# Attention scores for two heads at a time, and two weight chunks split ahead of a layer's last products: a two-block decoder on one Trainium2 core

## The chip, the core and the metric

The kernel runs as one program on one core of a Trainium2 chip. The metric is device time in microseconds (us), from the start of the program to its end. Below, TensorE is PE in the profile, VectorE is DVE, ScalarE is ACT, GpSimd is POOL, and SP is the engine whose queue issues the transfers.

## What is computed

256 tokens of width 1024 go through two blocks in float32. The first block is a mixer of three branches (short convolution, stick-breaking attention, retention), an attention over a memory of 256 rows and a squared-ReLU MLP. The second block has two layers with post-layer-norm: layer 0 is a state-space mixer and a convolutional FFN, layer 1 a latent attention (MLA) and the same kind of FFN. The parts that the change touches are the latent attention, the output products that end each sub-layer, and the norms behind them:

```python
def mla_shared_kv(h, kv_down_proj, kv_norm_g, kv_up_k, kv_up_v, cos, sin):
    ckv_kr = h @ kv_down_proj
    c_kv = rms_norm(ckv_kr[..., :MLA_KV_RANK], kv_norm_g)
    k_rope = apply_rope(ckv_kr[..., MLA_KV_RANK:], cos, sin)
    k_nope = (c_kv @ kv_up_k).reshape(b, s, 8, 128)
    v = (c_kv @ kv_up_v).reshape(b, s, 8, 128)

# for each block of 128 queries:
        scores = (jnp.einsum('bqhd,bkhd->bhqk', qn, k_nope)
                  + jnp.einsum('bqhr,bkr->bhqk', qr, k_rope)).astype(jnp.float32) * scale
        scores = jnp.where(key_idx[None, :] <= q_idx[:, None], scores, -jnp.inf)
        p = jax.nn.softmax(scores, axis=-1).astype(v.dtype)
        return jnp.einsum('bhqk,bkhd->bqhd', p, v)

def layer_norm(x, g, b):
    mu = jnp.mean(xf, axis=-1, keepdims=True)
    var = jnp.mean(jnp.square(xf - mu), axis=-1, keepdims=True)
    return (xf - mu) * lax.rsqrt(var + LN_EPS) * g + b
```

A score has a part over 128 features of its own head (nope) and a part over 64 rotary features whose keys all heads share (rope).

## The kernel before

**Tiles.** The 256 tokens are two token tiles (tau = 0 and 1) of 128. A float32 product is made of three products in fp32r: high part of the activations by high part of the weights, high by low, low by high (`mm3`, from line 672). In the profile these operands are `ah`, `al` (or `oTh`, `oTl`, `gTh`, `gTl`) and `wh`, `wl`.

**The weight stream.** The weights come as chunks in a fixed order. A chunk is transferred into `wr` (two buffers, `RAW`), ACT makes its high part with a CAST `wh<-wr` in two halves (`copy`, from line 523), and DVE makes its low part with a TENSOR_TENSOR `wl<-wr,wh`, again in two halves (`sub`, from line 537). When the second half is subtracted, the raw buffer is free, and `pump` issues the next transfer. Up to four prepared chunks are held (`HELD`): `can_prep` lets a chunk be split when it is transferred and fewer than four chunks lie between it and the last one that PE is done with. `get` hands a chunk to the products, `done` gives it back; `n_get`, `n_prep` and `n_done` count them.

**The order of the work** is settled when the program is built. A planner with a clock of its own runs the kernel's generators as tasks: `tick`, called between products, steps the tasks whose inputs it reckons ready, tasks marked `first` ahead of others, and `split_next` puts casts and subtractions between them, on the engine's reckoned idle time. What comes out is one list of instructions for each engine, and each engine takes its list in order. So an instruction that waits holds all that stands behind it on its engine.

**Layer ends.** `xstat` (from line 715) makes products whose moving side are the weights: output tiles of 128 tokens by up to 512 columns in two column blocks. The chunks that are not in the tail are used for both token tiles at once. The tail chunks (the last 2 to 4, `TAIL`) are used for tau 0 in a row, then for tau 1 in a row; in the last tail chunk the column blocks are done one after the other, and after block 0 a task is spawned that takes the result: `layernorm` (line 902) or an RMS norm. `layernorm` does, for each of two halves of 512 columns, a DVE SCALAR_TENSOR_TENSOR `x<-x,mm` (residual) and an ACT ACTIVATE `tk<-x,ln` (squares), then small DVE steps, a power on POOL, and two DVE SCALAR_TENSOR_TENSOR `x<-tk,rs,gb`; then PE transposes (`sm<-cst,x`, four to a PSUM bank), ACT casts them to `ah` and DVE subtracts to `al`. These two feed the next stage.

`xstat` with a task behind it ends six times: `wo` (after the mixers), `xo` (after the memory attention), `down` (after the MLP), `fd` (after the FFN of layer 0, and again of layer 1), `kvq` (the down projections of the latent attention, four chunks of 2 x 128 rows by 704 columns) and `ao` (its output). The next stage after `xo` is `up`, after layer 0's `fd` it is `kvq`, after `ao` it is `fu` (the FFN's first products). `up` and `fu` begin with three chunks that are used for tau 0, then for tau 1 (`wmixed`).

**Attention scores.** In `attention` (line 1784) each of the eight heads is a task `head(i)` (line 1924). It takes one PSUM bank of the `sm` group (four banks), makes the nope products (`sm<-knT,qnT`), adds the causal mask by two products (`sm<-maskb,identb`), makes the rope products, which use 64 of the 128 rows of the array (`sm<-krT,qrT`; even heads lie in rows 0 to 63, odd heads in rows 64 to 127), and then does the softmax on DVE and ACT, three transposes of `p`, and the product with `v`. Four heads are spawned after the query products of the first weight chunk, four after the second. `before(c)` holds chunk c of `ao` back until the heads of that chunk are done.

Nearly all instructions are recorded under one line, 284, that of a helper.

Of the kernel before, what the change touches and what calls it, by code (L numbers as in the profile page):

```python
# [471 lines left out]
class Kern:  # L472
# [86 lines left out]
    def done(self):  # L559
        self.n_done += 1  # L560

    def now(self):
# [155 lines left out]
    def xstat(self, tag, nks, lhs, blocks, tail=0, after=None, before=None):  # L720
# [29 lines left out]
        if tail:  # L750
            chs = []
            for tau in range(2):
                kk = k0
                if tau and ps[1] is None:
                    ps[1] = [self.bank() for _ in blocks]
                for c in range(tail):
                    if tau == 0:
                        if before:
                            before(len(nks) - tail + c)
                        chs.append(self.get(tag))  # L760
                    nk = nks[len(nks) - tail + c]
                    if c == tail - 1 and after:
                        got = [0]
                        for n in every:
                            part(chs[c], nk, kk, tau, [n])
                            got[0] += 1
                            if n == 0:
                                self.spawn(after(tau, ps[tau], got), first=True)
                            elif n < len(blocks) - 1:
                                self.tick()  # L770
                    else:
                        part(chs[c], nk, kk, tau, every)
                    kk += nk
                    if tau:
                        self.done()
                    else:
                        self.skew = 0.0 if c == tail - 1 else self.skew + nk * chs[c][0].shape[2] * UNIT / 2
                    self.tick()
# [1005 lines left out]
    def attention(self, h, act):  # L1784
# [4 lines left out]
        krT = pool.tile([P, S], F32, tag="krT", name="krT")  # L1789
        knT = pool.tile([P, 8, S], F32, tag="knT", name="knT")  # L1790
        qnT = pool.tile([P, 8, S], F32, tag="qnT", name="qnT")
        qrT = pool.tile([P, 4, S], F32, tag="qrT", name="qrT")
# [7 lines left out]
        for n, o in (("kvn", 0), ("qn", 256)):  # L1800
            b, w = ROWS[n]
# [119 lines left out]
        scale = 192 ** -0.5  # L1921
        obank = {}

        def head(i):
            sc = yield from self.sm.wait()
            r = slice(64 * (i % 2), 64 * (i % 2) + 64)
            self.mm1(sc[:, 0:128], qnT[:, i, 0:128], knT[:, i, 0:128], True)
            self.mm1(sc[:, 128:384], qnT[:, i, 128:256], knT[:, i, :], False)
            self.mm1(sc[:, 0:128], self.identb, self.maskb, False)
            self.mm1(sc[:, 256:384], self.identb, self.maskb, False)  # L1930
            self.mm1(sc[:, 0:128], qrT[r, i // 2, 0:128], krT[r, 0:128], False)
            self.mm1(sc[:, 128:384], qrT[r, i // 2, 128:256], krT[r, :], False)
            yield "dve"
            mx = self.tiny.tile([P, 2], F32, tag="mx", name="mx")
            nc.vector.tensor_reduce(mx[:, 0:1], sc[:, 0:128], axis=AX.X, op=MAX)
# [23 lines left out]
            c = slice(P * i, P * i + P)  # L1959
# [4 lines left out]
            yield from self.split((oT[0][:, i, :], oT[1][:, i, :]), po[:, :256])  # L1964
            self.sm.put(po)

        hs = []
        for b in (0, 4):
            self.wstat("qn", cq, 3, evac_to(qnT, b))
            self.until(*g_qr, *g_v)  # L1970
            for i in range(b, b + 4):
                hs.append(self.spawn(head(i)))
                self.tick()
        g_, b_ = self.bcast("lmg1", self.gb, "gb"), self.bcast("lmb1", self.gb, "gb")
        act = self.new_act()

        def before(c):
            self.until(*hs[:2 * c + 2])
        ps = self.xstat("ao", [2] * 4, self.lhs(oT), [(0, 512), (512, 1024)], tail=TAIL["ao"], before=before,
                        after=lambda t, p, got: self.layernorm(t, h, g_, b_, act, p, got))  # L1980
        close()
# [106 lines left out]
```

## Time and profile before

| | before |
|---|---|
| time, median of 3 runs | 1234.38 us (1233.92 to 1234.63) |
| the profiled execution: its own time | 1233.43 us |
| the profiled execution: its span | 1231.7 us |
| PE busy | 1214.2 us (99%) |
| DVE busy | 852.7 us (69%) |
| ACT busy | 718.0 us (58%) |
| all waits of PE on other work, as listed | 9.0 us |

The span runs from the first to the last instruction; 1.7 us of the execution's time lie outside it. The profiled execution is 0.95 us below the median of the runs. The busy time of PE is the union of its instructions, which overlap: a product of 256 columns is recorded with 0.28 us, and the next starts 0.117 us later.

### The profile page before, as it was taken

To read this page: it belongs to the slowest core of one execution; us is meant where nothing else is said; L and a number is where in the kernel's file an instruction comes from. 1 tells how busy PE (TensorE), PEld (TensorE's weight loads), DVE (VectorE), ACT (ScalarE), POOL (GpSimd) and SP (SyncE) were. 2 spreads that over 40 slices of the span, in tenths; PEclk is the share of its full clock that TensorE was granted. 3 is DMA by queue.
4 is the path that set the end of the run, shared out by engine and by line. 5 is a ranking of instruction groups with operands and counts; after the bars stand their busy time and mean duration, and the time that the engine had idled before them with its cause. 6 is when DMAs were issued, how large, how long until landed. Compare 5 with 4: busy or idle time off the path is not lost.

```text
span 1231.7 us, 20769 instructions
## 1 busy us (share of the span) xinstructions
PE 1214.2 (99%) x8468; PEld 1109.8 (90%) x8468; DVE 852.7 (69%) x1378; ACT 718.0 (58%) x1181; POOL 53.2 (4%) x85
## 2 busy tenths in 40 slices
PE   7999999999999999999999999999999999999997
PEld 5979999989989998888999898999988888999986
DVE  5666848677747765446887797888855866888853
ACT  5666546446536554345789765666643665666631
POOL 0011000000000000000111201000000000000000
PEclk9999999999999999999999999999999999999999
DMA  7643355546444556524556545555673442455560
GB/s 257 246 159 132 142 198 221 185 163 227 172 154 167 211 193 226 183 105 172 224 206 237 190 172 197 180 185 193 216 262 105 164 184 106 171 206 190 209 251 34
DMA packets 35425, 227.71 MB, mean 185 GB/s; under 512 B 4321, under 2 KB 4993, under 8 KB 11522
## 3 DMA queue, kind: packets, MB, share of 16 engines
q1 hardware_dynamic: 35330, 226.39, 51.1%
q8 instruction: 66, 1.08, 0.3%
q14 instruction: 29, 0.24, 0.1%
HBM read 225.27 MB, written 1.10 MB: 184 GB/s over the span
## 4 chain that ended last, share of the span: by engine, by line
PE 93%; DVE 3%; DMA 1%; ACT 1%; issue 0%; POOL 0%; SPq 0%; POOLq 0%; DVEq 0%; ACTq 0%
PE mm L284 84%; PE sm L284 9%; DMA wr<-wts 1%; DVE wl L284 1%; DVE x L284 1%; DVE tk L284 0%; POOL rs L284 0%; ACT wh L284 0%; SPq L284 0%; DVE dtw L284 0%; DVE ln L284 0%; DVE al L284 0%; ACT L284 0%; ACT tk L284 0%; POOLq L2084 0%
## 5 line engine op out<-in xcount | busy, mean ns | idle before, releaser
L284 DVE TENSOR_TENSOR wl<-wr,wh 128x1024 fp32r<-128x1024 f32 (+3 forms) x408 | 478.7, 1196 | 174.2 <-ACT wh L284 173.5
L284 ACT CAST wh<-wr 128x1024 fp32r<-128x1024 f32 (+3 forms) x408 | 403.9, 1030 | 160.4 <-PE mm L284 88.6
L284 PE MATMUL mm<-ah,wh 128*128 128x256 f32 (+1 forms) x1496 | 417.1, 279 | 0.0
L284 PE MATMUL mm<-ah,wl 128*128 128x256 f32 (+1 forms) x1496 | 413.6, 276 | 0.1
L284 PE MATMUL mm<-al,wh 128*128 128x256 f32 (+1 forms) x1496 | 413.4, 276 | 0.0
L284 PEld LDWEIGHTS mm<-ah,wh 128*128 128x128 f32 (+1 forms) x1496 | 280.2, 187 | 1.6 <-issue 1.1
L284 PEld LDWEIGHTS mm<-al,wh 128*128 128x128 f32 (+1 forms) x1496 | 280.3, 187 | 0.4
L284 PEld LDWEIGHTS mm<-ah,wl 128*128 128x128 f32 (+1 forms) x1496 | 280.2, 187 | 0.4 <-DVE wl L284 0.3
L284 DVE SCALAR_TENSOR_TENSOR r<-mm,pcol,r 128x255 f32<-128x255 f32 (+2 forms) x212 | 86.9, 474 | 35.1 <-ACT r L284 35.1
L284 PE MATMUL mm<-wl,ah 128*128 128x512 f32 (+3 forms) x320 | 106.1, 338 | 3.0 <-DVE wl L284 2.9
L284 PE MATMUL mm<-wh,ah 128*128 128x512 f32 (+3 forms) x320 | 108.7, 346 | 0.0
L284 PE MATMUL mm<-wh,al 128*128 128x512 f32 (+3 forms) x320 | 106.3, 338 | 0.5 <-DVE al L284 0.5
L284 PE MATMUL mm<-wh,gTh 128*128 128x512 f32 x304 | 96.2, 391 | 0.0
L284 PE MATMUL mm<-wl,gTh 128*128 128x512 f32 x304 | 95.6, 389 | 0.0
L284 PE MATMUL mm<-wh,gTl 128*128 128x512 f32 x304 | 95.5, 389 | 0.0
L284 ACT ACTIVATE r<-mm,pcol 128x256 f32<-128x256 f32 x96 | 48.9, 560 | 43.3 <-PE mm L284 43.3
L284 PEld LDWEIGHTS mm<-wl,ah 128*128 128x128 f32 x320 | 60.4, 190 | 10.0 <-DVE wl L284 4.6
L284 PEld LDWEIGHTS mm<-wh,gTl 128*128 128x128 f32 x304 | 57.1, 188 | 11.9
L284 PEld LDWEIGHTS mm<-wl,gTh 128*128 128x128 f32 x304 | 57.1, 188 | 11.8
L284 PEld LDWEIGHTS mm<-wh,gTh 128*128 128x128 f32 x304 | 56.7, 188 | 12.0 <-issue 0.6
L284 PEld LDWEIGHTS mm<-wh,al 128*128 128x128 f32 x320 | 60.2, 189 | 7.0 <-DVE al L284 1.2
L284 PEld LDWEIGHTS mm<-wh,ah 128*128 128x128 f32 x320 | 60.3, 189 | 6.5 <-issue 0.7
(296 smaller groups left out, 1576.6 us busy)
## 6 DMA issues: line engine op xcount, KB each, us to landing
wr<-wts SPq DMA_DIRECT2D x186, 1024.0 KB, 4.8
wr<-wts SPq DMA_DIRECT2D x11, 768.0 KB, 4.3
gb<-prow SPq DMA_DIRECT2D x12, 512.0 KB, 6.5
dec<-rows SPq DMA_DIRECT2D x8, 768.0 KB, 8.1
wr<-wts SPq DMA_DIRECT2D x4, 704.0 KB, 4.1
wr<-wts SPq DMA_DIRECT2D x4, 512.0 KB, 6.5
tk<-mem SPq DMA_DIRECT2D x2, 512.0 KB, 7.3
out<-x SPq DMA_DIRECT2D x4, 256.0 KB, 2.1
```

Source lines behind the costliest of these rows:

```text
L284: r = f(*args, **kw)
```

## The change

**Splits at layer ends.** A new function `ahead(n)` splits chunks at once, without the planner's rule on idle time, until n chunks beyond the one last handed out are prepared, or none can be. `xstat` calls `ahead(2)` in tau 1 in front of the last tail chunk's products, where a task follows. At the end of layer 1's `fd` no chunk is left, and at the end of `kvq` the order of the weight splits stays as it was.

**Scores.** Two heads become one task `scores(j)`. It waits for two `sm` banks, makes the nope products of both heads, then the masks of both, then the rope products of both, alternating between the two row groups. The two softmaxes are spawned as tasks `head(i, sc)` behind that.

The number of PE products is the same. Elsewhere (memory attention, the state-space mixer) the planner also puts some instructions in another order.

```diff
+    def ahead(self, n):
+
+        while self.n_prep < min(self.n_get + n, self.nch) and (self.subs or self.can_prep()):
+            self.sub() if self.subs else self.copy()
@@ xstat
                     if c == tail - 1 and after:
+                        if tau:
+                            self.ahead(2)
                         got = [0]
@@ attention
-        def head(i):
-            sc = yield from self.sm.wait()
-            r = slice(64 * (i % 2), 64 * (i % 2) + 64)
-            self.mm1(sc[:, 0:128], qnT[:, i, 0:128], knT[:, i, 0:128], True)
-            self.mm1(sc[:, 128:384], qnT[:, i, 128:256], knT[:, i, :], False)
-            self.mm1(sc[:, 0:128], self.identb, self.maskb, False)
-            self.mm1(sc[:, 256:384], self.identb, self.maskb, False)
-            self.mm1(sc[:, 0:128], qrT[r, i // 2, 0:128], krT[r, 0:128], False)
-            self.mm1(sc[:, 128:384], qrT[r, i // 2, 128:256], krT[r, :], False)
+        def scores(j):
+
+            scs = yield from self.sm.wait(2)
+            for e, sc in enumerate(scs):
+                i = 2 * j + e
+                self.mm1(sc[:, 0:128], qnT[:, i, 0:128], knT[:, i, 0:128], True)
+                self.mm1(sc[:, 128:384], qnT[:, i, 128:256], knT[:, i, :], False)
+            for sc in scs:
+                self.mm1(sc[:, 0:128], self.identb, self.maskb, False)
+                self.mm1(sc[:, 256:384], self.identb, self.maskb, False)
+            for q, k, o in ((slice(0, 128), slice(0, 128), slice(0, 128)), (slice(128, 256), slice(0, 256), slice(128, 384))):
+                for e, sc in enumerate(scs):
+                    r = slice(64 * e, 64 * e + 64)
+                    self.mm1(sc[:, o], qrT[r, j, q], krT[r, k], False)
+            for e, sc in enumerate(scs):
+                hs[2 * j + e] = self.spawn(head(2 * j + e, sc))
+
+        def head(i, sc):
             yield "dve"
...
-        hs = []
+        hs, pairs = {}, []
...
-            for i in range(b, b + 4):
-                hs.append(self.spawn(head(i)))
+            for j in range(b // 2, b // 2 + 2):
+                pairs.append(self.spawn(scores(j)))
...
         def before(c):
-            self.until(*hs[:2 * c + 2])
+            self.until(*pairs[:c + 1])
+            self.until(*[hs[i] for i in range(2 * c + 2)])
```

**Where layer 0 ends and `kvq` begins.** On ACT, the kernel before has the following. The `wh<-wr` casts of 704 columns are halves of `kvq`'s chunks, the `tk,ln<-x,ln` are the two squares of the layer norm of tau 1, and `ah` are the casts behind the transposes.

```order
L284 CAST wh<-wr 128x704 x3
L284 ACTIVATE ln<-ln 128x1
L284 ACTIVATE tk_9734,ln<-x,ln 128x512 x2
L284 ACTIVATE ln<-ln 128x1
L284 CAST wh<-wr 128x704 x2
L284 CAST ah<-sm_9808 128x4x128
L284 CAST ah<-sm_9818 128x4x128
L284 CAST wh<-wr 128x704 x2
```

And after the change, also on ACT:

```order
L284 CAST wh<-wr 128x704 x3
L284 ACTIVATE ln<-ln 128x1
L284 ACTIVATE tk_9735,ln<-x,ln 128x512
L284 CAST wh<-wr 128x704 x2
L284 ACTIVATE tk_9735,ln<-x,ln 128x512
L284 ACTIVATE ln<-ln 128x1
L284 CAST ah<-sm_9815 128x4x128
L284 CAST wh<-wr 128x704 x2
L284 CAST ah<-sm_9832 128x4x128
```

The two casts of `kvq`'s third chunk now stand between the two squares, and those of the fourth chunk ahead of the second `ah`.

On PE at the same place, the kernel before has this. `mm_9762` and its neighbour are the output of `kvq` for tau 0, and `sm<-cst,x` are the eight transposes of the layer norm of tau 1.

```order
L284 MATMUL mm_9762<-wl,ah 128x320
L284 MATMUL mm_9763<-wl,ah 128x384
L284 MATMUL mm_9762<-wh,al 128x320
L284 MATMUL mm_9763<-wh,al 128x384
L284 MATMUL sm_9808<-cst,x 128x128 x4
L284 MATMUL sm_9818<-cst,x 128x128 x4
L284 MATMUL mm_9762<-wh,ah 128x320
L284 MATMUL mm_9763<-wh,ah 128x384
L284 MATMUL mm_9762<-wl,ah 128x320
```

And after the change, from the first products of the third chunk on:

```order
L284 MATMUL mm_9766<-wh,ah 128x320
L284 MATMUL mm_9767<-wh,ah 128x384
L284 MATMUL mm_9766<-wl,ah 128x320
L284 MATMUL mm_9767<-wl,ah 128x384
L284 MATMUL mm_9766<-wh,al 128x320
L284 MATMUL mm_9767<-wh,al 128x384
L284 MATMUL sm_9815<-cst,x 128x128 x4
L284 MATMUL mm_9766<-wh,ah 128x320
L284 MATMUL mm_9767<-wh,ah 128x384
L284 MATMUL mm_9766<-wl,ah 128x320
```

Six products of the third chunk now stand ahead of the first four transposes, and six more ahead of the other four.

**Where `ao` ends and `fu` begins.** On DVE, the kernel before has this from the layer norm of tau 0 (its last two steps `x<-tk`) to that of tau 1. The `wl<-wr,wh` are halves of `fu`'s first chunks (those of the first one stand further ahead).

```order
L284 SCALAR_TENSOR_TENSOR x<-tk_10567,rs,gb 128x512 x2
L284 TENSOR_TENSOR al<-sm_10610,ah 128x4x128
L284 TENSOR_TENSOR al<-sm_10623,ah 128x4x128
L284 TENSOR_TENSOR wl<-wr,wh 128x1024
L284 SCALAR_TENSOR_TENSOR x,ln<-x,mm_10489 128x512
L284 TENSOR_TENSOR wl<-wr,wh 128x1024
L284 SCALAR_TENSOR_TENSOR x,ln<-x,mm_10490 128x512
```

And after the change, also on DVE:

```order
L284 SCALAR_TENSOR_TENSOR x<-tk_10557,rs,gb 128x512 x2
L284 TENSOR_TENSOR wl<-wr,wh 128x1024 x2
L284 TENSOR_TENSOR al<-sm_10614,ah 128x4x128
L284 TENSOR_TENSOR al<-sm_10621,ah 128x4x128
L284 TENSOR_TENSOR wl<-wr,wh 128x1024 x2
L284 SCALAR_TENSOR_TENSOR x,ln<-x,mm_10483 128x512
L284 SCALAR_TENSOR_TENSOR x,ln<-x,mm_10484 128x512
```

Four subtractions of weights now stand between the end of the one layer norm and the first residual step of the other, where one stood.

## Rows read from the trace of the kernel before

**Rows 1.** Page, part 1: busy time, share of the span, instructions

```profile
PE 1214.2 (99%) x8468; PEld 1109.8 (90%) x8468; DVE 852.7 (69%) x1378; ACT 718.0 (58%) x1181; POOL 53.2 (4%) x85
```

**Rows 2.** Waits of PE: total us, times, longest us

```profile
PE mm L284 <- DVE wl L284: 2.9, 3, 1.8
```

**Rows 3.** Timeline of PE, head scores (start, us, operation, tile, shape, [idle before])

```profile
989.88 0.82 PE L284 MATMUL sm<-knT,qnT 128*128 128x128 f32 x4
990.53 0.28 PE L284 MATMUL sm<-maskb,identb 128*128 128x128 bf16 x2
990.74 0.92 PE L284 MATMUL sm<-krT,qrT 64*128 64x128 f32 x4
991.59 0.92 PE L284 MATMUL sm<-knT,qnT 128*128 128x128 f32 x4
```

**Rows 4.** Timeline of PE, scores of two heads of the first block's attention

```profile
47.87 0.92 PE L284 MATMUL sm<-qT,kT 64*128 64x256 f32 x8
48.72 0.50 PE L284 MATMUL mm<-wh,ah 128*128 128x512 f32 x1
```

**Rows 5.** Timeline of DVE, end of the first head's softmax

```profile
993.94 0.55 DVE L284 TENSOR_SCALAR p<-p,sm 128x128 f32<-128x128 f32 x2
```

**Rows 6.** Timeline of ACT, end of layer 0

```profile
950.51 0.72 ACT L284 ACTIVATE tk<-x,ln 128x512 f32<-128x512 f32 x1 [0.36 <-DVE x L284]
...
951.42 1.45 ACT L284 CAST wh<-wr 128x704 fp32r<-128x704 f32 x2
```

**Rows 7.** Timeline of SP, end of layer 0: issue of the third kvq chunk

```profile
947.18 0.33 SPq L284 DMA_DIRECT2D wr<-wts  x1
```

**Rows 8.** Page, part 6: count, KB each, median us from issue to landing

```profile
wr<-wts SPq DMA_DIRECT2D x186, 1024.0 KB, 4.8
...
wr<-wts SPq DMA_DIRECT2D x4, 704.0 KB, 4.1
```

**Rows 9.** Timeline of DVE, end of layer 0

```profile
953.09 1.41 DVE L284 SCALAR_TENSOR_TENSOR x<-tk,rs,gb 128x512 f32<-128x512 f32 x2 [0.44 <-POOL rs L284]
...
957.22 1.68 DVE L284 TENSOR_TENSOR wl<-wr,wh 128x704 fp32r<-128x704 f32 x2
```

**Rows 10.** Timeline of PE, start of kvq

```profile
953.89 1.38 PE L284 MATMUL sm<-cst,x 128*128 128x128 f32 x8 [0.34 <-DVE x L284]
...
958.96 0.42 PE L284 MATMUL mm<-wl,ah 128*128 128x320 f32 x1
```

**Rows 11.** Timeline of DVE, end of the memory attention (xo)

```profile
377.02 1.42 DVE L284 SCALAR_TENSOR_TENSOR tk<-x,rs,gb 128x512 f32<-128x512 f32 x2 [0.73 <-POOL rs L284]
```

**Rows 12.** Timeline of PE, end of the first block (down)

```profile
552.77 0.50 PE L284 MATMUL mm<-wh,al 128*128 128x512 f32 x1 [0.45 <-DVE al L284]
```

**Rows 13.** Timeline of DVE, end of ao

```profile
1038.20 1.21 DVE L284 TENSOR_TENSOR wl<-wr,wh 128x1024 fp32r<-128x1024 f32 x1
1039.33 0.68 DVE L284 SCALAR_TENSOR_TENSOR x<-x,mm 128x512 f32<-128x512 f32 x1
...
1044.39 1.41 DVE L284 SCALAR_TENSOR_TENSOR x<-tk,rs,gb 128x512 f32<-128x512 f32 x2 [0.45 <-POOL rs L284]
```

**Rows 14.** Timeline of PE, start of fu

```profile
1045.20 1.38 PE L284 MATMUL sm<-cst,x 128*128 128x128 f32 x8
...
1046.99 0.39 PE L284 MATMUL mm<-wl,ah 128*128 128x256 f32 x1 [0.29 <-DVE wl L284]
```

**Rows 15.** Timeline of PE, first products and the last one

```profile
8.48 1.97 PE L284 MATMUL sm<-cst,tk 128*128 128x128 f32 x8 [2.25 <-DVE tk L284]
...
13.58 0.43 PE L284 MATMUL mm<-wl,ah 128*128 128x512 f32 x1
...
16.94 0.50 PE L284 MATMUL mm<-wl,ah 128*128 128x512 f32 x1 [1.79 <-DVE wl L284]
...
1223.33 0.39 PE L284 MATMUL mm<-wh,gTl 128*128 128x512 f32 x1
```

**Rows 16.** Windows: us, busy us of each engine, granted clock, DMA share, GB/s

```profile
1228.80:1231.70 2.90, 0.00 (x0) 0.00 (x0) 0.00 (x0) 0.00 (x0) 0.00 (x0) 0.50 0.45 167
```

## The prediction, made before the changed kernel ran

> **What bounds the kernel now.** I read the page's busy times first: PE is busy for 1214.2 us of 1231.7, 99% [rows 1]. PE's own list of waits comes next, and it is short: the waits for low weight parts `wl` add up to 2.9 us in three places [rows 2], of which one, 1.79 us, lies at the start of the kernel [rows 15]. So there are two ways to change the time: PE's work must shrink, or a wait must open or close. DVE and ACT have idle time on the average, but that is no evidence for a layer end. There the norm of the second token tile is a chain over DVE, ACT and POOL of some 6 us, and PE stays busy only because enough products stand ready in its list to cover it. In the windows at `kvq` and `fu` the cover just reaches: PE starts the transposes 0.34 us late at 953.89 [rows 10] and waits 0.29 us for `wl` at 1046.99 [rows 14]. Whatever delays the chain there by more than some tenths of a us is paid in full. So I took the new order of each engine at these places and went through it with the durations of the trace.
>
> **Part 1, paired scores.** One head costs PE 0.65 us for the nope products, 0.21 for the masks and 0.85 for the rope products (from start to start: 989.88, 990.53, 990.74, 991.59) [rows 3], with a switch of banks 1.8 a head. The trace has the paired form elsewhere: in the first block's attention, products of 64 rows for two heads, on both row groups in turn, fill 0.85 us (47.87 to 48.72) [rows 4], as much as one head's rope products in [rows 3], though the record counts eight pieces and not four. So the second head's rope products should cost next to nothing: minus 0.85 a pair, and about 0.1 more since the array changes between 128 and 64 rows once instead of twice. Four pairs: -3.8 us at the most; 0 if the row groups do not overlap here. The cost: a head's softmax starts when both heads' scores are done, while DVE and ACT serve one head after the other. Before, the first head's `p` was done 3.8 us after the end of its scores, at 994.49 [rows 5]. In the new order the transposes of `p` for two heads stand where the second softmax has only just ended; going through the two groups of four heads I find PE waiting 0.6 and 0.7 us. Net -2.5 us up to the last products of `ao`.
>
> [...]
>
> **Part 2, splits at the end of layer 0 (`fd` to `kvq`).** Now the two casts of `kvq`'s third chunk stand on ACT between the two squares of the norm. Before, ACT was free at 950.15, the second square ran at 950.51, and the casts came after it at 951.42 [rows 6]. They could not have come sooner: the chunk's transfer was issued at 947.18 [rows 7] and takes 4.1 us to land [rows 8], so it is there at 951.28. The issue hangs on a subtraction that the change leaves where it is. So ACT, which takes its list in order, now stands waiting for the transfer from 950.1 to 951.3, casts for 1.45, and the second square starts at 952.8 instead of 950.5: +2.27 us. All that hangs on the square moves along: the norm's last step `x<-tk` ends at 956.77 instead of 954.50 [rows 9]. The low part of the third chunk stands behind it on DVE and has its first half at 957.6. PE's new order has six products of that chunk ahead of the transposes; the third of them needs this half, so PE stands from 953.7 to 957.6, 3.9 us, with the transposes still to do. Behind it, `ah`, the casts of the fourth chunk, `al` and its subtractions follow as before; the last half of the fourth chunk's `wl` is there at 961.97 instead of 958.90 (957.22 plus 1.68) [rows 9], and the product that waits for it starts at 962.0 instead of 958.96 [rows 10]. **+3.06 us.** Bounds: 0 if the transfer landed before 950 (2.9 us after its issue; nothing in [rows 8] is that fast), 4 if it lands a us late.
>
> **Part 3, the end of `ao`.** PE arrives 2.5 us sooner here through part 1. But DVE's list is now full: between the norm of tau 0 and the first residual step of tau 1 stand four weight subtractions, where one stood. `x<-tk` of tau 0 ends at about 1033.8; four subtractions (1.15 from start to start, 1.21 alone [rows 13]) and two `al` (0.62) are 5.8 us, so the residual step starts at 1039.5. Before it was 1039.33 [rows 13], with PE 2.5 us later: the gain of the pairs is gone by then. Next, the casts of `fu`'s third chunk stand between the squares here too. Its transfer is issued about 1036.1 and lands 4.8 us later [rows 8], so the casts run from 1040.9 to 1042.9 and the second square at 1043.1 instead of 1041.8. With the 2.6 us from that square to `x<-tk` (1044.39) [rows 13], `x` is done at 1047.1 and the chunk's first low half at 1048.2. PE, in its new order, reaches the product that needs it at about 1042.5, waits 5.7 us, and still has the eight transposes to do (1.13 us, from 1045.20 to 1046.33), which before were done when the same product started at 1046.99 [rows 14]. So 1048.2 + 1.1 - 1047.0 = **+2.3 us**, all of part 1 included. Bounds: -2.5 if the chain waits for nothing new, +4 if the transfer is a us or more later.
>
> **Part 4, the other ends.** `wo`: products of the memory's keys lie behind it and cover everything; 0. `xo`: two subtractions of 1.2 us now stand ahead of an `al` and of the residual steps; the norm's last step slips by 0.7 from 377.02 [rows 11], and three products of the third `up` chunk stand ahead of the transposes; PE waits some **+0.85 us** for its `wl`. `down`: a subtraction of 1.2 stands ahead of the residual step, so the `al` for which PE already waits (552.77) [rows 12] comes **+0.55 us** later. Each of the two lies between 0 and 1.2, one subtraction. The new order in the memory attention and in the state-space mixer moves instructions on engines for which PE does not wait there; I take 0, with 0.7 us either way for each.
>
> **Sum:** 3.06 + 2.3 + 0.85 + 0.55 = 6.8, less 0.2 to 0.3 for a wait of 0.3 us after `fu`'s start that the later weights should swallow: +6.5 us. On the profiled execution's own 1233.4 that is 1239.9; the median of the runs is 0.95 above it, and against the median, 1234.4, I forecast **1240.9 us**.
>
> **Rivals.**
> (a) The clock falls as well. [...] The idle of 1.79 us before 16.94 cost no clock: the products behind it run at full pace. [...] From the first product at 8.48 to the rise at about 13.6 [rows 15] there were 5.1 us of work at half pace, so a fall costs about 2.6 us: 1243.5. [...]
> (b) The chains at `ao` are no later than before, since PE's lead lets the transfers start sooner as well: then the pairs' 2.5 us stay, and 3.06 + 0.85 + 0.55 - 2.5 = +2.0: 1236.4, within what can be told from no change.
> (c) Faster: the casts find their chunks landed and hold no square. Then both layer ends pay nothing, the waits for `wl` behind the kernel's start close (2.9 less 1.8, 1.1 us [rows 2, 15]), and the pairs give -2.5: 1230.8. It decides at one point, whether `kvq`'s third chunk lands before 950, when ACT comes to it. For it speaks that these splits were the last thing PE waited for at both places; against it, [rows 7, 8].
> (d) The pairs give nothing, because the two row groups do not overlap with these shapes: PE then comes to the end of `ao` 1.3 us later than before instead of 2.5 earlier, and the chain behind the transfer sets the end all the same: +8 to +9, about 1243. [rows 4] speaks against it.
>
> **How the numbers follow.** Forecast 1240.9 with a chance of 0.40; (a) 0.24, (b) 0.15, (c) 0.11, (d) and the reordered mixers 0.10. What a measurement can tell from no change is 0.2%, 2.5 us, so 1231.9 to 1236.9. Faster is (c), with 0.01 of the low end of (b): 0.12. Same is (b) and a forecast with `kvq` or `fu` at the low bound: 0.16. Slower is the rest: 0.72. The range drops (c) and the far end of (a) and (d): the forecast's bounds (0.85 and 0.55 to 0, the mixers -1.4, a transfer faster by half a us at both places) reach down to about 1236, (b) to 1235; upwards (a) with a late transfer reaches 1245.
>
> **What the profile would show.** Part 1: eight records of rope products for a pair in about 0.85 us, and a pair in 2.7 us instead of 3.6. Part 2: on ACT the square, casts that wait for the transfer, then the second square, and PE idle by some 3.9 us in front of a `wl` product of 320 columns. Part 3: DVE without a gap ahead of the residual step, and PE idle by some 5.7 us in front of a `wl` product of 256 columns; the granted clock tells (a). What would make it wrong: a transfer that lands sooner than 4.1 us after its issue, or an issue that is moved ahead.

## The result

| | before | after |
|---|---|---|
| time, median of 3 runs | 1234.38 us (1233.92 to 1234.63) | 1243.78 us (1243.58 to 1244.02) |
| ratio to before, 95% interval | | 1.0079 (1.0065 to 1.0092) |
| span of the profiled execution | 1231.7 us | 1241.8 us |
| mean granted clock of PE | 0.999 | 0.994 |

The change makes the kernel 9.4 us slower. The page of after, part 1, answers to [rows 1]:

```profile
PE 1214.8 (98%) x8468; PEld 1112.0 (90%) x8468; DVE 855.5 (69%) x1378; ACT 716.1 (58%) x1179; POOL 46.6 (4%) x85
```

PE's busy time is the same within 0.6 us, though the pairs saved some and though PE ran at half pace for 6.0 and 3.4 us (below): on balance, what was added is idle time. PE's waits of after (what it waited for; us in total, times, longest) answer to [rows 2]:

```profile
PE mm L284 <- DVE wl L284: 11.5, 6, 5.0
...
PE sm L284 <- DVE x L284: 1.6, 3, 1.0
PE mm L284 <- ACT ah L284: 0.7, 1, 0.7
```

The waits for low weight parts went from 2.9 to 11.5 us, and two of them make 8.7.

**The start of `kvq`.** The timeline of ACT, after (start, us, operation, tile, shape, in brackets the idle time ahead and what ended it), answers to [rows 6]:

```profile
952.76 0.72 ACT L284 ACTIVATE tk<-x,ln 128x512 f32<-128x512 f32 x1
...
954.62 1.46 ACT L284 CAST wh<-wr 128x704 fp32r<-128x704 f32 x2 [1.04 <-DMA wr<-wts]
955.98 0.72 ACT L284 ACTIVATE tk<-x,ln 128x512 f32<-128x512 f32 x1
```

ACT does the first square, stands for 1.04 us until the transfer has landed, casts, and only then does the second square, 3.2 us behind the first one; before, it was 1.2 us (949.34 and 950.51). The timeline of PE there answers to [rows 10]:

```profile
956.52 0.48 PE L284 MATMUL mm<-wh,ah 128*128 128x320 f32 x2
960.68 0.95 PE L284 MATMUL mm<-wl,ah 128*128 128x320 f32 x2 [3.67 <-DVE wl L284]
961.43 0.79 PE L284 MATMUL mm<-wh,al 128*128 128x320 f32 x2
962.02 1.05 PE L284 MATMUL sm<-cst,x 128*128 128x128 f32 x4
```

The products behind the idle stretch take longer than those ahead of it: 0.79 to 0.95 us recorded for a pair, against 0.48. The windows of after (us, busy time of PE, PEld, DVE, ACT and POOL, granted clock, DMA share, GB/s) show why, and answer to [rows 16]:

```profile
959.50:960.00 0.50, 0.00 (x0) 0.00 (x0) 0.50 (x2) 0.00 (x0) 0.00 (x0) 0.83 0.00 0
960.00:960.70 0.70, 0.02 (x1) 0.02 (x1) 0.70 (x2) 0.00 (x0) 0.00 (x0) 0.50 0.00 0
...
966.50:967.00 0.50, 0.50 (x4) 0.50 (x4) 0.50 (x1) 0.00 (x0) 0.00 (x0) 0.84 0.00 0
```

The granted clock fell to 0.50 at about 959.8 and came back at about 966.7. PE worked for 6.0 us of that (960.68 to 966.7). At half pace that is 3.0 us lost at the most; by e9 below, in which the clock stays up and PE waits for other work instead, it cost 1.5 us.

**The start of `fu`.** The timeline of ACT at the norm of tau 1, after:

```profile
1047.62 0.72 ACT L284 ACTIVATE tk<-x,ln 128x512 f32<-128x512 f32 x1
...
1048.34 1.98 ACT L284 CAST wh<-wr 128x1024 fp32r<-128x1024 f32 x2
1050.22 0.71 ACT L284 ACTIVATE tk<-x,ln 128x512 f32<-128x512 f32 x1
```

And of DVE and of PE, answering to [rows 13, 14]:

```profile
1044.33 2.35 DVE L284 TENSOR_TENSOR wl<-wr,wh 128x1024 fp32r<-128x1024 f32 x2
1046.60 0.68 DVE L284 SCALAR_TENSOR_TENSOR x<-x,mm 128x512 f32<-128x512 f32 x1
```

```profile
1055.26 0.48 PE L284 MATMUL mm<-wl,ah 128*128 128x256 f32 x1 [5.00 <-DVE wl L284]
1055.54 0.42 PE L284 MATMUL mm<-wh,al 128*128 128x256 f32 x1
1055.76 1.05 PE L284 MATMUL sm<-cst,x 128*128 128x128 f32 x4
```

DVE goes without a gap from the subtractions to the residual step; the squares have casts between them, but here no wait for a transfer; PE is idle for 5.0 us, and the clock falls a second time, now 0.1 to 0.2 us after PE has gone on, until about 1058.8 (granted clock 0.63 in the window from 1055.20 to 1056.00, 0.80 in that from 1058.00 to 1060.00). That is 3.4 us of work at half pace; by e9 it cost 1.6 us.

**The pairs.** The timeline of PE, after, answers to [rows 3]:

```profile
997.43 1.47 PE L284 MATMUL sm<-knT,qnT 128*128 128x128 f32 x8
998.74 0.39 PE L284 MATMUL sm<-maskb,identb 128*128 128x128 bf16 x4
999.06 0.93 PE L284 MATMUL sm<-krT,qrT 64*128 64x128 f32 x8
999.91 1.58 PE L284 MATMUL sm<-knT,qnT 128*128 128x128 f32 x8
```

A pair takes 2.48 us from start to start (the second one 2.60), where the same two heads took 3.52 (the next two 3.63), and its rope products take 0.85.

**Where the time went.** Both records hold the same 8468 products on PE, and the same product stands at the same place in the count within a hundred. So the difference between the starts of products with the same number tells how late PE is, and the growth of that difference over a stretch tells what the stretch cost. Times in the head are those of the kernel before; the last column is the sum. The rows e1 to e12 are the experiments below; in e7 and e9 the added products are left out of the count.

| us against before | to 248 | 248 to 927: `wo`, `xo`, `down`, mixer | 927 to 990: end of `fd`, `kvq` | 990 to 1035: attention | 1035 to 1061: end of `ao`, `fu` | to the end |
|---|---|---|---|---|---|---|
| changed kernel | -0.15 | +2.92 | +4.78 | -2.81 | +5.60 | +10.30 |
| e1 pairs alone | +0.12 | -0.19 | -0.01 | -2.80 | +6.10 | +3.22 |
| e2 splits alone | -0.84 | +1.46 | +4.28 | 0.00 | +0.90 | +5.79 |
| e3 without those at `fd` | -0.07 | +1.52 | +0.36 | -2.85 | +5.61 | +4.52 |
| e4 without those at `ao` | -0.26 | +2.25 | +4.51 | -2.76 | +4.39 | +8.11 |
| e5 pairs, one subtraction | -0.10 | -0.05 | +0.02 | -3.64 | +4.57 | +0.76 |
| e6 and cover at `ao` | +1.05 | -0.16 | +0.04 | -3.64 | +0.05 | -2.67 |
| e7 useless products | -0.56 | +2.51 | +4.23 | -2.76 | +5.61 | +9.00 |
| e8 e6, rope in sequence | +0.34 | -0.24 | +0.03 | -3.62 | +1.03 | -2.46 |
| e9 more of them | +0.67 | +1.48 | +3.24 | -2.81 | +4.02 | +6.56 |
| e10 changed, one subtraction | -0.03 | +1.61 | +4.58 | -3.62 | -0.23 | +2.31 |
| e11 e6 with `wo`, `xo`, `down` | +1.13 | +2.47 | +0.38 | -3.64 | +0.02 | +0.35 |
| e12 e6 again | -0.66 | -0.23 | +0.01 | -3.64 | +0.03 | -4.50 |

The first column is not the change's: e6 and e12 are the same kernel and have +1.05 and -0.66 there, and PE's wait for `tk` at the start is 2.4 us in the one and 1.4 in the other. Nor is all of the stretch from 1035 on: at its end PE waits for a copy (`tk`) on ACT, which in the kernel before has stood 0.80 us for a transfer, for 0.2 us in that kernel, 0.98 in e1, 0.73 in e2 and 1.2 in e8, although e8 differs from e6, with 0.23 us, in the order of the rope products alone.

### The profile page after: what moved, and what is told of

The parts are those of the page before. It is cut to its first block, busy times and chain, and to the rows that moved or that the text cites. A ratio compares the mean times of both kernels' runs of the same rounds, so it can differ in the third digit from the quotient of the medians.

```text
span 1241.8 us, 20758 instructions
## 1 busy us (share of the span) xinstructions
PE 1214.8 (98%) x8468; PEld 1112.0 (90%) x8468; DVE 855.5 (69%) x1378; ACT 716.1 (58%) x1179; POOL 46.6 (4%) x85
## 4 chain that ended last, share of the span: by engine, by line
PE 90%; DVE 4%; ACT 2%; DMA 1%; issue 1%; POOL 1%; SPq 0%; POOLq 0%; DVEq 0%; ACTq 0%
PE mm L284 82%; PE sm L284 9%; DVE wl L284 2%; DVE x L284 1%; DMA wr<-wts 1%; ACT wh L284 1%; POOL rs L284 1%; ACT tk L284 1%; DVE tk L284 0%; DMA cst<-cst 0%; ACT p L284 0%; ACT ah L284 0%; DVE ln L284 0%; DVE al L284 0%; ACT dec L284 0%
```

## The experiments

Each median stands beside that of the kernel before on the same chip.

**e1: pairs alone** (the changed kernel without the call of `ahead`).

```diff
-                        if tau:
-                            self.ahead(2)
```

> Paired scores alone, without the splits at layer ends; the program is that of before up to the scores at about 990. My theory (the gain of the pairs is real, but the norm behind ao sets the time there): PE is 2.5 to 3 us ahead at the end of ao, then waits some 2 to 3 us behind the norm of tau 1, because the order there still has two subtractions and two casts of fu's first chunk in the norm of tau 0; in all 1233.5 to 1235 us. Rival (the gain of the pairs stays): 1231.5 to 1232. Rival (the row groups do not overlap): rope products of a pair take 1.7 us, and 1235 or more.

Measured: 1236.14 us against 1233.64, ratio 1.0019 (1.0010 to 1.0028): slower than before. The first theory has the right place, and its price was too low by at least 1 us; it had left out the clock, which falls here too (0.55 in the window from 1043.50 to 1046.00). PE is 2.8 us ahead at the end of `ao` and loses 6.1 behind it, 0.8 of that in the wait for ACT's copy named above, so about as much as the whole change does there. The timeline of ACT at the norm of tau 0, and of PE at `fu`'s second chunk, in e1:

```profile
1026.88 0.72 ACT L284 ACTIVATE tk<-x,ln 128x512 f32<-128x512 f32 x1
...
1027.60 1.98 ACT L284 CAST wh<-wr 128x1024 fp32r<-128x1024 f32 x2
1029.48 0.72 ACT L284 ACTIVATE tk<-x,ln 128x512 f32<-128x512 f32 x1
```

```profile
1039.53 0.28 PE L284 MATMUL mm<-wh,ah 128*128 128x256 f32 x1
1043.55 0.43 PE L284 MATMUL mm<-wl,ah 128*128 128x256 f32 x1 [3.74 <-DVE wl L284]
```

The casts of `fu`'s first chunk hold the norm of tau 0, and the low part of the second chunk stands behind the norm of tau 1: PE has 24 products ahead of the transposes and not 48. So the loss at `fu` is there without a single early split. Why the stream is late shows on DVE and SP. The kernel before:

```profile
989.61 2.36 DVE L284 TENSOR_TENSOR wl<-wr,wh 128x1024 fp32r<-128x1024 f32 x2 [4.88 <-ACT wh L284]
```

```profile
1009.04 0.33 SPq L284 DMA_DIRECT2D wr<-wts  x1
```

And e1, DVE with the second half alone:

```profile
997.17 1.22 DVE L284 TENSOR_TENSOR wl<-wr,wh 128x1024 fp32r<-128x1024 f32 x1
```

```profile
1021.73 2.93 SPq L284 DMA_DIRECT2D wr<-wts  x2
```

The second half of a weight subtraction, which the kernel before has at 990.75 and right behind the first half, is put behind the softmax steps of two pairs, 6.4 us later, although DVE was idle from 990.75 to 992.38. Its raw buffer comes free so much later: the next transfer goes out at 998.45 and not at 991.99, and two transfers on, that of `fu`'s first chunk goes out at 1021.73, where the kernel before issues it at 1009.04.

**e2: splits alone** (the kernel before with `ahead` and its call).

> The splits at layer ends alone, scores one head after the other. My theory: the idle at kvq with its fall of the clock is there as in the changed kernel (+4.6), also the 2.7 us that had gathered before 940; at ao the third chunk's casts stand behind the second square, as in the kernel before, so the idle of 5 us is not there: about 1241.5 to 1242.5. Rival (the splits cost the 5.8 us at ao by themselves): 1247 to 1248.

Measured: 1239.02 us against 1233.64, ratio 1.0048 (1.0036 to 1.0061). Below the forecast, and far below the rival: 4.3 us at `kvq`, 1.5 ahead of 927, and 0.9 behind `ao`. Of the 0.9 us, 0.55 is the wait for ACT's copy named above. The early splits at `ao` cost next to nothing by themselves.

**e3: no early splits at the end of the FFN.**

```diff
-                        if tau:
+                        if tau and tag != "fd":
```

> The changed kernel, but without the early splits at the end of the FFN (fd); the order at the start of kvq is that of the kernel before there. My theory: the idle of 3.7 us, the fall of the clock behind it and the 0.9 us of slow start go, the rest stays, also the idle at fu: 1239 to 1239.5. Rival (the loss is in the reordering of many places, and PE only waits elsewhere instead): above 1241.5.

Measured: 1239.19 us against 1233.64, ratio 1.0046 (1.0032 to 1.0059), as forecast. The stretch at `kvq` costs 0.4 us instead of 4.8. PE's timeline, e3, has the old wait there (0.77 us in the kernel before):

```profile
959.97 0.42 PE L284 MATMUL mm<-wl,ah 128*128 128x320 f32 x1 [0.78 <-DVE wl L284]
```

**e4: no early splits at the end of `ao`** (`tag != "ao"` in the same place).

> The changed kernel, but without the early splits at the end of ao. The casts of fu's third chunk then stand behind the second square. My theory: the idle of 5 us in front of fu's third chunk and the fall of the clock go (5.8 us), but a wait of 2 to 3 us in front of the transposes is left, as with the pairs alone: 1240 to 1242. Rival (DVE's full list sets the time at ao, not the squares): the idle stays near 5 us, 1243 or more.

Measured: 1241.76 us against 1233.64, ratio 1.0066 (1.0054 to 1.0079). The time is in the range of the first theory, but not for its reason: the idle of 5.0 us became one of 3.7 in front of the second chunk, and the clock falls behind that one as well (0.63 in the window from 1050.00 to 1053.00). Only 1.2 of the 5.6 us went with the splits:

```profile
1050.09 0.39 PE L284 MATMUL mm<-wl,ah 128*128 128x256 f32 x1 [3.66 <-DVE wl L284]
```

**e5: pairs alone, with the pending subtraction in front of them.**

```diff
+            while self.subs:
+                self.sub()
             for j in range(b // 2, b // 2 + 2):
                 pairs.append(self.spawn(scores(j)))
```

> Paired scores alone, and in front of the pairs the one weight subtraction that is still pending on DVE is done at once (with the pairs alone it stood behind two pairs' softmaxes, so its chunk's raw buffer came free, and the next transfer went out, 6.5 us later). Theory: that one place is why the stream of weights is a chunk late at the end of ao; now the transfer of fu's first chunk goes out before 1010 instead of at 1021.7, its casts no longer stand between the squares of the norm of tau 0, the idle in front of fu's second chunk falls from 3.7 to about 2.4 us and the clock stays up: 2.5 to 3.5 us faster than the pairs alone, so about the time of before (within 1 us). Rival (the place of this subtraction does not matter): within 0.5 us of the pairs alone, 1236.

Measured: 1233.81 us against 1233.97, ratio 1.0002 (0.9993 to 1.0011), 2.3 us below e1 (2.7 where each is taken against the kernel before on its own chip). DVE and SP, e5:

```profile
989.48 2.36 DVE L284 TENSOR_TENSOR wl<-wr,wh 128x1024 fp32r<-128x1024 f32 x2 [4.87 <-ACT wh L284]
```

```profile
1016.88 3.88 SPq L284 DMA_DIRECT2D wr<-wts  x2
```

The transfer of `fu`'s first chunk goes out at 1016.88, 4.9 us sooner than in e1 but not before 1010, and the norm of tau 0 is free of casts. The idle in front of the second chunk did not fall to 2.4 us, it is 3.45, and the clock still falls behind it (0.61 in the window from 1042.30 to 1044.00, 0.50 in the next to 1046.00). So the place of this one subtraction matters as forecast, and it is not the whole cause. What is left of the delay has the same shape one chunk on: the second half of the next chunk is cast behind the softmax steps of the second group of heads, where the kernel before has both its casts at 1004.52, and the edit takes pending subtractions alone. ACT, e5:

```profile
1013.20 1.10 ACT L284 CAST wh<-wr 128x1024 fp32r<-128x1024 f32 x1
```

**e6: the cover at `ao` as well** (added to e5). The subtractions of `fu`'s second chunk are put around the first residual step of tau 1, as in the kernel before.

```diff
+                    if tag == "ao" and tau and c == 2:
+                        self.ahead(2 if self.n_prep > self.n_get else 1)
```

> As the one before, and at ao the subtractions of fu's second chunk are put around the first residual step of tau 1, as the kernel before has them, so that PE has 48 products and not 24 ahead of the transposes. Theory: then nothing waits longer than in the kernel before, and the whole gain of the pairs is left: 2.5 to 3 us below before, 1230.5 to 1231.5. Rival (DVE is full behind the norm of tau 0, and any two subtractions ahead of the residual step hold it): 1233 or more, with the wait in front of the transposes.

Measured: 1230.34 us against 1233.97, ratio 0.9967 (0.9955 to 0.9979): faster than both kernels. The gain of 3.6 us that the pairs made up to the end of `ao` is still there at the end. PE at `fu`, e6:

```profile
1042.65 1.21 PE L284 MATMUL sm<-cst,x 128*128 128x128 f32 x7
1043.62 0.36 PE L284 MATMUL mm<-wh,ah 128*128 128x256 f32 x1
1044.28 0.38 PE L284 MATMUL mm<-wl,ah 128*128 128x256 f32 x1 [0.30 <-DVE wl L284]
```

This is the picture of [rows 14], with the same wait of 0.3 us.

**e10: the whole change, with the pending subtraction in front of the pairs** (the edit of e5 in the changed kernel).

> The whole change, with the one pending subtraction done in front of the pairs. Theory: the loss at ao comes from the stream being a chunk late behind the pairs, not from the splits ahead of the last products; the early splits at ao stay, their casts now come behind the second square, PE has 48 products of cover, the idle of 5 us is gone: 5 to 6 us below the changed kernel, 1237.5 to 1239, with the loss at kvq left. Rival (the early splits at ao hold the norm whenever they are there): 1241 or more.

Measured: 1236.54 us against 1233.67, ratio 1.0019 (1.0010 to 1.0028), 6.5 to 7.2 us below the changed kernel (against before on the same chip, and directly), a little better than forecast. The call at `ao` is there, and the stretch behind `ao` costs nothing (-0.2). In this kernel's list for ACT the casts of `fu`'s third chunk stand behind the second square, although the call was made ahead of it. ACT and PE, e10:

```profile
1044.67 0.71 ACT L284 ACTIVATE tk<-x,ln 128x512 f32<-128x512 f32 x1
...
1045.56 1.98 ACT L284 CAST wh<-wr 128x1024 fp32r<-128x1024 f32 x2
```

```profile
1049.70 0.39 PE L284 MATMUL mm<-wl,ah 128*128 128x256 f32 x1 [0.30 <-DVE wl L284]
```

PE waits 0.30 us and not 5.0, and the next product, at 1049.92, is recorded with 0.28 us, as products of 256 columns are at full pace; at half pace it was 0.41 (the changed kernel at 1056.82).

**e7 and e9: useless work against the fall of the clock.** Ahead of `kvq`'s third chunk and of `fu`'s third, PE does n products of zeros and an identity (bf16, 128 columns) into a free bank, without the planner's clock being told, so that the lists of all other engines stay as they are; n is 20 and 32 in e7, 46 and 76 in e9.

```diff
+    def keep(self, n):
+        pt = self.sm.get()
+        for _ in range(n):
+            self.nc.tensor.eng.matmul(pt[:, 0:128], lhsT=self.identb, rhs=self.maskb, start=True, stop=True, ...)
+        self.sm.put(pt)
...
+                    if tag == "kvq" and tau == 0 and c == 2:
+                        self.keep(20)
...
+                if tag == "fu" and self.late and tau == 0 and c == 2:
+                    self.keep(32)
```

> The changed kernel with useless work added on PE alone: 20 products of 128 columns (bf16, into a free bank) ahead of kvq's third chunk, 32 ahead of fu's third chunk; nothing else is moved, no wait is taken away. They fill some 1.2 to 2 us and 2 to 3.5 us of the two idle stretches. [...] Rival (the slow products behind the two gaps have another cause than the idle, or it is the time since the gap's start that counts): 1243 to 1245.

Measured, e7: 1242.15 us against 1233.97, ratio 1.0066 (1.0054 to 1.0079), 1.2 to 1.6 us below the changed kernel, where I had expected 4 to 5 us with the clock staying up: a product of this kind takes 0.056 us, not the 0.06 to 0.11 that I had reckoned with, and idle stretches of 2.26 and 3.20 us were left. The windows, e7:

```profile
959.00:959.50 0.50, 0.00 (x0) 0.00 (x0) 0.50 (x2) 0.00 (x0) 0.00 (x0) 1.00 0.00 0
959.50:960.00 0.50, 0.37 (x1) 0.37 (x2) 0.50 (x2) 0.00 (x0) 0.00 (x0) 0.51 0.00 0
...
1054.50:1055.00 0.50, 0.50 (x7) 0.50 (x5) 0.50 (x1) 0.04 (x1) 0.00 (x0) 1.00 0.00 0
1055.00:1056.00 1.00, 1.00 (x8) 1.00 (x7) 0.48 (x2) 0.54 (x1) 0.00 (x0) 0.54 0.00 0
```

The clock fell in both places all the same. At `kvq` it was low for less time (959.5 to 962.9), and the stretch cost 0.55 us less than in the changed kernel; at `fu` nothing was gained. So e9 leaves less idle time:

> As the kernel with useless PE work in front of the two idle stretches, with more of it: 46 products ahead of kvq's third chunk and 76 ahead of fu's third, at 0.056 us each (the run before showed that) 2.6 and 4.3 us, so that 1.1 and 0.8 us of idle are left. With the smaller filling, idle of 2.3 and 3.2 us was left and the clock still fell at both places. Theory (the idle makes the clock fall): now it stays up at both, and the time is 4 to 5 us below the changed kernel: 1238.5 to 1240. Rival (the length of the idle does not matter): 1241 or more.

Measured, e9: 1239.63 us against 1233.67, ratio 1.0052 (1.0038 to 1.0066), 3.4 to 4.2 us below the changed kernel, with 122 more products. The timeline of PE at `kvq`, and windows over both places:

```profile
955.89 2.74 PE L977 MATMUL sm<-maskb,identb 128*128 128x128 bf16 x46
958.44 0.56 PE L284 MATMUL mm<-wh,ah 128*128 128x320 f32 x2
959.91 0.59 PE L284 MATMUL mm<-wl,ah 128*128 128x320 f32 x2 [0.91 <-DVE wl L284]
```

```profile
953.00:962.00 9.00, 8.09 (x81) 7.64 (x81) 5.06 (x10) 3.06 (x7) 0.99 (x1) 1.00 0.37 122
...
1046.00:1054.00 8.00, 7.29 (x101) 7.05 (x100) 5.28 (x8) 3.07 (x7) 0.93 (x1) 1.00 0.32 123
1054.00:1060.00 6.00, 6.00 (x54) 6.00 (x52) 3.93 (x5) 3.23 (x5) 0.00 (x0) 1.00 0.52 180
```

With idle stretches of 0.9 and 0.7 us the clock stays at 1.00, and nothing else was changed. This settles that the slow products come from the idle time. Their price is read best from the two stretches of the table: 4.78 less 3.24 and 5.60 less 4.02, so 1.5 and 1.6 us, 3.1 together. The 3.4 to 4.2 us between the medians are somewhat more, and the two records differ ahead of `kvq` too, where nothing was changed (2.92 and 1.48 us up to 927); the work at half pace in the changed kernel's own windows would be 4.7 us if no wait stood behind it.

**e8: rope products one head after the other** (e6 with the two loops exchanged; one run).

```diff
-            for q, k, o in (...):
-                for e, sc in enumerate(scs):
+            for e, sc in enumerate(scs):
+                for q, k, o in (...):
```

> As the cover kernel, with the rope products of a pair in the order of before, both of head 0 and then both of head 1, instead of alternating. Theory (what gains is that neighbouring instructions lie on different row groups): only the middle two overlap, and a pair's rope products take 1.2 to 1.5 us instead of 0.85; 1.5 to 2.5 us slower in all. Rival (the array runs ahead over several instructions, or it is the fewer changes of row groups that gain): 0.85 as in the alternating order, or 1.7 and no gain at all.

Measured: 1230.79 us, and a pair's rope products in 0.87 us, so the theory falls. (Of the time, 1.0 us more than in e6 is the wait for ACT's copy named under the table.) PE, e8:

```profile
991.32 0.39 PE L284 MATMUL sm<-maskb,identb 128*128 128x128 bf16 x4
991.63 0.93 PE L284 MATMUL sm<-krT,qrT 64*128 64x128 f32 x8
992.50 1.58 PE L284 MATMUL sm<-knT,qnT 128*128 128x128 f32 x8
```

The single records show the same: the first product of the second head starts 0.013 us after that of the first head, although an instruction of 256 columns lies between them in the program; in the changed kernel it is 0.006 us. By this one run it is enough that the two heads' rope products are neighbours; alternating them gains next to nothing (0.85 against 0.87 us).

**e11 and e12: the three ends ahead of 927.** e11 is e6 with `ahead(2)` at the ends of `wo`, `xo` and `down`; e12 is e6 again on the same chip.

> The cover kernel (paired scores with the subtraction in front and the cover at ao) with the early splits at the ends of wo, xo and down added, and nowhere else. Theory: these three ends and the new order that they cause in the memory attention and the state-space mixer are the 1.5 us by which PE was late at 940 in the kernels with early splits; the cost stays to the end, since nothing behind it has slack: 1.2 to 2 us above the cover kernel, 1231.5 to 1232.5. Rival (it is swallowed where PE waits anyway): within 0.5 us of the cover kernel.

> The cover kernel again, beside the one with three early splits, so that the two have the same chip: 1230 to 1231, 2.5 to 4 us below the kernel before.

Measured: e11 1232.71 us, ratio 0.9988 (0.9980 to 0.9997); e12 1229.61 us, ratio 0.9966 (0.9952 to 0.9979); both against 1233.98. The three ends cost 3.1 us, more than the 1.2 to 2 that I forecast. In the records it is 2.47 against -0.23: 0.65 us at 381 (`xo`) and 0.3 more than before at 554 (`down`), where the waits were forecast, 0.7 at 601 and 0.8 more at 764 in the state-space mixer, where the planner's order moved, and the rest in many small places. The wait at 764, for the residual step's `x`, is 0.93 us in e11 and 0.99 in the changed kernel, but 0.15 in e2, e3 and e10, which have the same splits there; what makes it long in some records stays open.

## Why the prediction was right, and where it was wrong

The forecast was 1240.9 us with a range of 1235 to 1245; measured were 1243.78. The direction, the two main places and the chains of waits there held; the time is that of rival (a), 1243.5, to which I gave 0.24. That it fits to 0.3 us is in part luck: without the clock, the pairs and `ao` came out 1.1 us below their forecast and the other ends 1.5 above theirs, and the clock fell in two places for 3.1 us and not once for 2.6.

**Right, to tenths: the chain at `kvq`.** I had put the second square at 952.8 on the time scale of before; PE came there 3.1 us late, so 955.9, and it started at 955.98. The end of `x<-tk` was forecast at 956.77 + 3.1 = 959.87; it is 959.83 (a step of 1.42 us started at 958.41). PE's product was forecast at 957.6 + 3.1 = 960.7 behind an idle time of 3.9 us; it started at 960.68 behind 3.67. Without the clock's 1.5 us the stretch cost 3.2 us (forecast 3.06). e3 shows that the place is the cause. A chain at a layer end can be worked out in advance from the order of the lists and the durations of the trace.

**Wrong size: the clock, in both places and not in the sum.** In the trace of before, the granted clock is 0.50 from 1228.80 on [rows 16], and the last product ends at 1223.7 [rows 15]. I took these 5.1 us of idle time as the point from which the clock falls, so that `kvq` with 3.9 seemed half safe; `fu` with 5.7 lay above it, so by my own reading a fall there belonged in the sum, and I left it to a rival. The changed kernel fell at `kvq` 2.8 us after the last product had ended, and e7 fell with an idle stretch of 2.26 us. One row from the end of a trace was an upper bound, and I used it as a threshold; the only safe row was the 1.79 us at the start. e9 prices the step at 3.1 us by the table, 3.4 to 4.2 by the medians. The forecast sum of 6.5 with that is 9.6 to 10.7; measured are 9.4, and 10.1 between the profiled executions.

**Right chain, wrong cause: the loss at `ao` (part 3).** As a chain of waits in the changed kernel, part 3 was near: the product that waits was forecast at 1048.2 on the time scale of before; PE was 7.55 us late at 990, and it started at 1055.26, which is 1047.7 on that scale. Parts 1 and 3 together were forecast at +2.3 us, and the two stretches are -2.81 and +5.60, of which 1.6 is the clock, so +1.2 without it. But I laid it on the early splits: on DVE's list of four subtractions and on the third chunk's casts between the squares. e1 has neither the call nor those casts and loses 6.1 us there; e2 has the call and loses 0.9; e10 has the call and the pairs and, with one subtraction moved, loses nothing. The cause is the pairs: the planner puts the second half of one weight subtraction behind the softmax steps of two pairs, the weight stream runs late by that, and the chunks of `fu` arrive where the norms stand. With the pairs alone, moving that subtraction mends little (e5 still loses 4.6 us), and the cover of e6 is needed as well; in the changed kernel the early splits at `ao` give that cover (e10). The step that failed is the second sentence of part 3 ("DVE's list is now full"): I compared the lists at `ao` and asked what had been added there, and not why the subtractions came so late. The list of SP tells it: the transfer of `fu`'s first chunk, 12.7 us later in e1. The outcome of rival (b), that the pairs' gain stays, is what e6 shows once that is mended; its reason, transfers that start sooner, is borne out only in part, since that first transfer still goes out later there than before (1017.93 against 1009.04).

**The wait for the transfer at `ao`** was not there: the casts at 1048.34 follow the first square without a gap. The transfer, issued at 1043.28, took 4.7 us and had landed 0.35 us before. The second square came 1.9 us late by the casts alone. The working had no room for a wait either: a residual step at 1039.5 puts the end of the first square at about 1041.2 (by the 1.74 us between the two in the trace of before), behind the landing at 1040.9.

**The pairs** gave 2.81 us net of waits (forecast 2.5), and 3.64 where the subtraction is done in front. A pair costs 2.48 or 2.60 us, not the 2.7 of the forecast: the nope products of two heads in a row take 1.31 us, and the second set of masks 0.1. That the row groups overlap was read rightly from [rows 4], and (d) falls. In the changed kernel, the rope products of both heads take 0.85 us, as those of one head did. The 0.1 us a pair for the change between 128 and 64 rows shows in the traces too: the nope products take 0.65 us behind products of 128 rows (before, 989.88 to 990.53) and 0.76 behind the rope products of 64 (991.59 to 992.35), in the changed kernel 1.31 and 1.42 for two heads. It is not the switch of banks that part 1 names: the nope products of two heads lie in two banks and take 1.31 us, twice 0.65.

**The other ends** were forecast at 1.4 us with `xo` at 0.85 and `down` at 0.55; they are 0.65 and 0.3, and the reordered mixer, taken as 0 within 0.7, costs about 1.5. Together 2.9 in the changed kernel, and 2.7 in e11.

**Rival (c)** was the one on the other side. Its condition, that the third chunk of `kvq` lands before ACT comes to it, is refuted by the row: ACT waited 1.04 us for the transfer.

## What to carry to other kernels

At a layer end, a cast or a subtraction for later work that is put ahead of a step of the norm costs not only its own duration (1.9 us at `ao`) but also the wait that it brings along (1.04 us at `kvq`), and where PE then stands idle, the clock's fall can come on top (at `kvq`, behind 3.67 us of idle time, 1.5 us on 3.2); so ask of each instruction put ahead whether its transfer has landed when its engine comes to it. When a change frees PE and the time does not move, look at when the transfers are issued: one subtraction that slips behind a burst of other work holds a buffer, and that comes out 50 us later at another place. The remedy here was one line that does the pending subtraction in front of the burst and one that keeps the old cover: with both, and without the early splits, the pairs make the kernel 0.33% faster.

## What the runs showed of the hardware that I had not expected

- In e7 the clock fell once with PE at work again and once with PE idle. PE was idle for 3.20 us up to 1053.97, the granted clock was still 1.00 in the window from 1054.50 to 1055.00, with PE busy throughout, and 0.54 on the average of the next microsecond. At `kvq` it fell at about 959.5, with PE idle from 957.37 to 959.63. Behind idle stretches of 0.91 and 0.71 us (e9) the granted clock stayed at 1.00, and behind the one of 1.79 us (before, [rows 15]) the products of 512 columns from 17.28 on are recorded with 0.39 to 0.48 us, against 0.63 at half pace (12.30).
- How long PE works at half pace differs as well: 6.0 us at `kvq` and 3.4 at `fu` in the same execution of the changed kernel.
- Products of 64 rows for two heads run side by side even when two products of one head stand ahead of those of the other (e8): 0.87 us for a pair against 0.85.
